# Seven products in place of eight in layer 0's channel MLP as well, with the order of its chunks changed

## The chip, the cores and the metric

The kernel runs on one core of a Trainium2 chip. Its engines work side by side, each through its own instructions in program order: TensorE (PE in the profile; its weight loads are PEld) multiplies, VectorE (DVE) and ScalarE (ACT) do the elementwise work, GpSimd (POOL) does nearly nothing here, and SyncE (SP) issues the DMAs. Operands lie in SBUF, matmul results in PSUM, everything large in DRAM. The metric is the device time of one execution in microseconds, shown as the median of three runs with the lowest and the highest.

## The reference, cut to what matters

Two layers; the first mixes with a spatial gating unit, the second with a pooling mixer. Both end in the same channel MLP, which is where the change lies.

```python
D_MODEL = 1024; SEQ = 1024; DEC_SEQ = 32; D_FF = 4 * D_MODEL
...
    for i in range(DEPTH):
        mod = jax.nn.silu(c) @ w_ada[i] + b_ada[i]
        sh1, sc1, gt1, sh2, sc2, gt2 = jnp.split(mod[:, None, :], N_MOD, axis=-1)
        h = rmsnorm(x, g_norm[i, 0]) * (1 + sc1) + sh1
...
        x = x + gt1 * rmsnorm(mix, g_norm[i, 1])
        h = rmsnorm(x, g_norm[i, 2]) * (1 + sc2) + sh2
        f = jnp.square(jax.nn.relu(h @ ffn_w_up[i])) @ ffn_w_down[i]
        x = x + gt2 * rmsnorm(f, g_norm[i, 3])
```

It runs for 1024 prompt frames and 32 sample frames that share the weights. All arrays are float32.

## The kernel before

**Tiles and splits.** Activations lie transposed, channels on the partitions, frames along the free axis, in three tiles: tiles 0 and 1 hold 384 prompt frames each, tile 2 the last 256 and the 32 sample frames, 288 columns. `acc[t]` holds a tile's residual stream. Every float32 operand is split in a high part (`wh`, `hh`, `fh`) and the remainder (`wl`, `hl`, `fl`), and each product is three matmuls: high by high, high by low, low by high (`products`, L923 to L925). ScalarE rounds the high part, VectorE subtracts for the low one. So a weight load of 128x1024 costs one activation (L419) and one VectorE subtraction, and each hidden block a relu, a square (ScalarE) and a split.

**The channel MLP** runs in chunks of 512 hidden features: `ffn_item` makes four up blocks `pf` (24 matmuls each) and leaves eight down blocks `pg` (12 each), which are issued after the next item's first up block (`pending`, `flush`). `accumulate` has VectorE add each `pg` to `acc`. After a tile's last chunk `Stat` sums squares for the next norm, and the caller's `after` starts a chain (`to_pool` after layer 0, `to_out` after layer 1).

**Seven products.** In layer 1 the last four chunks (`COMBINED = 4`) of tiles 0 and 1 are taken together by `combined_item`: a two-by-two scheme over even and odd blocks of channels and of hidden features, seven products of 12 matmuls (L1588) in place of eight, twice a chunk. It needs sums of the weights (`sh`, `sl`, made by `do_s`) and sums of the columns of the two tiles. The latter are made by `sums_of_columns` and `other_sums` out of the modulated activations that `mix_to_ffn` has stored in DRAM (`md`). They, and more hidden pieces, lie in the SBUF of tile 2's activations, in two of the sixteen weight slots (`W_SLOTS`, `w_cap`) and in borrowed buffers; `acc[2]` serves as scratch. When the last combined chunk's up products are issued, `late_modulation` loads tile 2 back from `md[2]` and remakes its `hh` and `hl`.

**The order of passes** (`passes`, L321 to L328). Layer 0: chunks 0 and 1 tile by tile, chunks 2 and 3 each over all three tiles with the weights loaded once, then chunks 4 to 7 of tile 0, of tile 1, of tile 2. Layer 1: chunks 0 to 3 of tile 0, of tile 1, the four combined ones, then all eight of tile 2.

**What else is woven in.** `fillers` is a queue of generators: the chains between the channel MLP and the next mixer (`ffn0_t`, `ffn1_t`, `out_t`) and the column sums. `weave`, called between blocks, pulls from the first two as long as a running estimate of VectorE's time (`time["dve"]`) is behind that of TensorE, and `finish` forces one to its end: `run_ffn` does so in front of a tile's first chunk. The modulation vectors come from `w_ada` by VectorE (`add_ada`, `add_wide`: scale and add into `aa`, transpose, reduce); these ada items stand in one stream with the weight loads, and `some_ada` says after which pass how many. The loop `for n, (l, c, tiles) in enumerate(passes)` puts twelve into each of layer 0's shared chunks and four into each of chunks 4 to 7 of tile 0. `stream_ready` holds a load back until there is a weight slot; from 24 loads in front of the first combined chunk (`wtight`) it counts `w_cap`, 14 slots, 16 after the last.

**The layers' border.** `to_pool(st)` appends `run`: the residual, scaling by `coef`, window sums, four groups of pooling matmuls `pp` (L2015) whose weights `wg` are loaded in front of each, and `mix_to_ffn`, whose `apply` makes eight scalings, `hh` and `hl`.

## Time and profile before

| | us |
|---|---|
| median of three runs | 2155.68 (2154.72 to 2156.45) |
| the profiled execution | 2157.29, its span 2155.4 |
| mean granted TensorE clock | 0.998 of full speed |

By stages, from the profile's windows (busy time in us):

| stage | from to | PE | DVE | ACT |
|---|---|---|---|---|
| norms and gating mixer | 0 to 577 | 571.86 | 392.65 | 224.31 |
| channel MLP of layer 0 | 577 to 1402 | 823.97 | 607.77 | 402.42 |
| layer 1, plain chunks of tiles 0 and 1 | 1402 to 1681.6 | 276.32 | 222.37 | 162.77 |
| its four combined chunks | 1681.63 to 1935.39 | 252.71 | 141.40 | 115.88 |
| tile 2 and the end | 1935.39 to 2155.4 | 210.02 | 144.33 | 111.20 |

A row of the windows gives start:end, length, the busy time of each engine with the number of instructions, the granted clock, the DMA share and GB/s. A row of the timeline gives start, duration, engine, line, operation, output and inputs, and in brackets the idle time before it and what ended it. Nearly every VectorE operation bears the line of one helper, L80, so it is told apart by its tiles. Matmuls are pipelined: a 384-column one lasts 0.33 us in the rows, and the next starts sooner. Line numbers are those of the kernel before.

### The profile page before, as it was taken

The numbers are of one execution on the slowest core, as the hardware profiler recorded it, in microseconds if no ns is written. First come the engines' busy times: TensorE is split into PE (matmuls) and PEld (weight loads), VectorE is DVE, ScalarE is ACT, GpSimd is POOL, SyncE is SP. The second block draws the span as 40 slices with busy tenths as digits, with TensorE's granted clock in tenths as the row PEclk, the third lists the DMA queues.
The fourth block names the chain that finished last, engine by engine and source line by source line (L and its number), as shares of the span: only waits on it lengthen the run. The fifth ranks groups of instructions, "written<-read, shape, count | busy, mean of one in ns | idle before, by whom it ended". The sixth has DMA issues, their size and how long they took to land.

```text
span 2155.4 us, 33342 instructions
## 1 busy us (share of the span) xinstructions
PE 2134.9 (99%) x13137; PEld 2060.1 (96%) x13137; DVE 1508.5 (70%) x2665; ACT 1016.6 (47%) x1738; POOL 15.3 (1%) x34
## 2 busy tenths in 40 slices
PE   9999999999999999999999999999999999999998
PEld 6778999999999999999999999999999999999998
DVE  6787748557778558486887868887858655479464
ACT  5534322234456552323345566666556443366454
POOL 0000000000000000000000000000000000001000
PEclk9999999999999999999999999999999999999999
DMA  8487524253447454243665546755556222158572
GB/s 307 147 266 214 164 86 127 86 161 107 135 120 225 126 151 147 87 138 115 198 187 152 163 143 210 221 171 177 156 172 188 79 69 69 40 164 228 146 204 79
DMA packets 393394, 330.02 MB, mean 153 GB/s; under 512 B 39986, under 2 KB 355930, under 8 KB 393236
## 3 DMA queue, kind: packets, MB, share of 16 engines
q1 hardware_dynamic: 392564, 326.99, 49.9%
q8 instruction: 103, 1.69, 0.3%
q0 software_dynamic: 640, 0.88, 0.1%
q14 instruction: 55, 0.45, 0.1%
q10 hardware_dynamic: 32, 0.01, 0.0%
HBM read 291.67 MB, written 36.17 MB: 152 GB/s over the span
## 4 chain that ended last, share of the span: by engine, by line
PE 87%; DVE 5%; DMA 4%; ACT 2%; issue 1%; SPq 0%; DVEq 0%; ACTq 0%
PE pg L923 10%; PE pg L925 10%; PE pg L924 10%; PE pf L923 8%; PE pf L924 8%; PE pf L925 8%; PE po L923 3%; PE po L925 3%; PE po L924 3%; PE pu L923 3%; PE pu L925 3%; PE pu L924 3%; PE pv L951 2%; PE pv L950 2%; PE pv L952 2%; PE pf_0a L1588 2%
## 5 line engine op out<-in xcount | busy, mean ns | idle before, releaser
L923 PE MATMUL pg<-fh,wh_dn 128*128 128x384 f32 (+1 forms) x1440 | 462.8, 322 | 0.2
L924 PE MATMUL pg<-fl,wh_dn 128*128 128x384 f32 (+1 forms) x1440 | 461.0, 320 | 1.7 <-DVE fl L80 1.5
L925 PE MATMUL pg<-fh,wl_dn 128*128 128x384 f32 (+1 forms) x1440 | 460.1, 320 | 0.0
L923 PE MATMUL pf<-hh,wh_up 128*128 128x384 f32 (+1 forms) x1280 | 409.2, 320 | 0.2 <-ACT r L1511 0.2
L924 PE MATMUL pf<-hl,wh_up 128*128 128x384 f32 (+1 forms) x1280 | 407.5, 319 | 0.8 <-DVE hl L80 0.8
L925 PE MATMUL pf<-hh,wl_up 128*128 128x384 f32 (+1 forms) x1280 | 407.3, 318 | 0.2 <-DVE wl_up L80 0.2
L924 PEld LDWEIGHTS pg<-fl,wh_dn 128*128 128x128 f32 x1440 | 270.3, 188 | 3.6 <-DVE fl L80 2.8
L923 PEld LDWEIGHTS pg<-fh,wh_dn 128*128 128x128 f32 x1440 | 270.2, 188 | 2.7 <-DVE acc L80 1.3
L925 PEld LDWEIGHTS pg<-fh,wl_dn 128*128 128x128 f32 x1440 | 270.2, 188 | 0.0
L80 DVE TENSOR_TENSOR wl_up<-raw,wh_up 128x1024 fp32r<-128x1024 f32 (+1 forms) x168 | 186.6, 1119 | 105.0 <-ACT wh_up L419 104.3
L80 DVE TENSOR_TENSOR acc<-acc,pg 128x384 f32<-128x384 f32 (+1 forms) x336 | 172.2, 517 | 111.6 <-PE pg L925 110.5
L419 ACT ACTIVATE wh_up<-raw 128x1024 fp32r<-128x1024 f32 x144 | 152.2, 1058 | 191.3 <-PE pf L924 118.7
L924 PEld LDWEIGHTS pf<-hl,wh_up 128*128 128x128 f32 x1280 | 240.2, 188 | 1.5 <-DVE hl L80 1.0
L925 PEld LDWEIGHTS pf<-hh,wl_up 128*128 128x128 f32 x1280 | 240.6, 188 | 0.6 <-DVE wl_up L80 0.6
L419 ACT ACTIVATE wh_dn<-raw 128x1024 fp32r<-128x1024 f32 x160 | 169.0, 1058 | 152.8 <-PE pg L924 101.9
L923 PEld LDWEIGHTS pf<-hh,wh_up 128*128 128x128 f32 x1280 | 240.0, 188 | 1.1 <-ACT r L1511 0.4
L80 DVE TENSOR_TENSOR wl_dn<-raw,wh_dn 128x1024 fp32r<-128x1024 f32 x160 | 195.4, 1222 | 58.2 <-ACT wh_dn L419 48.8
L80 DVE SCALAR_TENSOR_TENSOR aa<-raw,csil,aa 128x512 f32<-128x512 f32 (+1 forms) x364 | 203.2, 619 | 6.6 <-DMA raw<-in_w_ada_dram 6.5
L1511 ACT ACTIVATE r<-pf 128x384 f32<-128x384 f32 (+1 forms) x160 | 71.3, 446 | 176.6 <-PE pf L925 174.0
L923 PE MATMUL pu<-hh,wh_u 128*128 128x384 f32 (+1 forms) x384 | 125.8, 328 | 0.0
L923 PE MATMUL po<-ush,wh_o 128*128 128x384 f32 (+1 forms) x384 | 123.6, 322 | 0.0
L925 PE MATMUL pu<-hh,wl_u 128*128 128x384 f32 (+1 forms) x384 | 123.4, 321 | 0.0
(471 smaller groups left out, 3548.6 us busy)
## 6 DMA issues: line engine op xcount, KB each, us to landing
raw<-in_ffn_w_up_dram SPq DMA_DIRECT2D x160, 512.0 KB, 4.0
raw<-in_ffn_w_down_dram SPq DMA_DIRECT2D x160, 512.0 KB, 3.5
raw<-in_w_ada_dram SPq DMA_DIRECT2D x96, 512.0 KB, 4.5
raw<-in_sgu_w_in_dram SPq DMA_DIRECT2D x40, 512.0 KB, 4.2
xd<-acc SPq DMA_DIRECT2D x8, 1536.0 KB, 7.6
raw<-in_sgu_w_out_dram SPq DMA_DIRECT2D x24, 512.0 KB, 3.7
xo_r<-xd SPq DMA_DIRECT2D x32, 384.0 KB, 4.1
vd<-vt SPq DMA_DIRECT2D x32, 256.0 KB, 4.5
```

Source lines behind the costliest of these rows:

```text
L80: return op(out, *args, **kw)
L419: act(out=wh, in_=r, func=AF.Copy)
L923: mm(ps[:, :n], wh, rh, start=i == 0, stop=False)
L924: mm(ps[:, :n], wh, rl, start=False, stop=False)
L925: mm(ps[:, :n], wl, rh, start=False, stop=i == last)
L950: mm(ps[:m, :], a_h, wh[:, o : o + 512], start=k == 0, stop=False)
L951: mm(ps[:m, :], a_h, wl[:, o : o + 512], start=False, stop=False)
L952: mm(ps[:m, :], a_l, wh[:, o : o + 512], start=False, stop=k == KB - 1)
L1511: act(out=r[:, :n], in_=ps[:, :n], func=AF.Relu)
L1588: mm(ps[:, :n], u, v, start=first and k == 0 and x == 0, stop=k == 3 and x == 2, skip_group_check=True,)
```

## The change

Both layers now have a range of combined chunks, `COMBINED = [range(2, 6), range(4, 8)]`. In each layer tile 0 runs all its plain chunks, tile 1 those below the range, then come the combined ones, tile 1's chunks above the range, and tile 2's eight. In layer 0 that is tile 0: 0, 1, 6, 7; tile 1: 0, 1; both: 2 to 5; tile 1: 6, 7; tile 2: 0 to 7. In layer 1 the order is as it was. The twenty weight chunks of each layer stay twenty. `ends` says which pass is a tile's last, whatever its chunk number.

`mix_to_ffn` now stores the modulated activations in layer 0 too. `sums_of_columns` makes all four sums of columns, in the places where tile 0's `hh` and `hl` lay (the two tiles change roles in the products), once tile 0's plain chunks are issued (`plain`) and the chains of tiles 0 and 1 are done. Three weight slots are taken in place of two, and `aa` is no longer borrowed. A combined block waits for the second half of its weights only behind the first half of its first product. The remaining ada items move: two in each plain pass of tile 1 in layer 0, six in each combined chunk there, two in each of layer 1.

```diff
 W_SLOTS = 16
-COMBINED = 4
+COMBINED = [range(2, 6), range(4, 8)]
 RAW_SLOTS = 3
...
     every = list(range(NT))
-    passes = [(0, c, [t]) for t in every for c in (0, 1)]
-    passes += [(0, c, every) for c in range(2, 4)]
-    passes += [(0, c, [t]) for t in every for c in range(4, 8)]
     pair = every[:-1]
-    passes += [(1, c, [t]) for t in pair for c in range(8 - COMBINED)]
-    passes += [(1, c, pair) for c in range(8 - COMBINED, 8)]
-    combined = range(len(passes) - COMBINED, len(passes))
-    passes += [(1, c, [NT - 1]) for c in range(8)]
+    passes = []
+    runs = []
+    for l, cs in enumerate(COMBINED):
+        low, high = range(cs[0]), range(cs[-1] + 1, 8)
+        passes += [(l, c, [0]) for c in (*low, *high)] + [(l, c, [1]) for c in low]
+        runs.append(range(len(passes), len(passes) + len(cs)))
+        passes += [(l, c, pair) for c in cs]
+        passes += [(l, c, [1]) for c in high] + [(l, c, [NT - 1]) for c in range(8)]
+    ends = {(l, t): n for n, (l, _, tiles) in enumerate(passes) for t in tiles}
+    plain = set()
+    begun = set()
+    combined = [n for r in runs for n in r]
...
         w_chunk(n)
-        if l == 0:
-            some_ada(12 if len(tiles) > 1 else 4 if c >= 4 and tiles == every[:1] else 0)
+        if n in combined:
+            some_ada(2 if l else 6)
+        elif l == 0 and tiles == [1]:
+            some_ada(2)
     assert not rest
...
     wpos = {k: i for i, k in enumerate(worder)}
-    wtight = min(wpos[s[1]] for s in stream if s[0] == "s") - 24
+    wtight = [min(wpos[s[1]] for s in stream if s[0] == "s" and s[1][1] in r) - 24 for r in runs]
     wdone = set()
...
-    w_cap = [W_SLOTS - 2]
+    w_taken = [3, 3]
...
             i = wpos[stream[k][1]]
-            if i < wtight:
+            if stream[k][0] == "s" and passes[stream[k][1][1]][0] not in begun:
+                return False
+            if i < wtight[0]:
                 return i < W_SLOTS // 2 or worder[i - W_SLOTS // 2] in wdone
             used = sum(cost(key) for key in worder[:i] if key not in wdone)
-            return used + cost(worder[i]) <= w_cap[0]
+            return used + cost(worder[i]) <= W_SLOTS - max(
+                n for n, first in zip([0] + w_taken, [0] + wtight) if i >= first
+            )
         return True
...
                 flush()
-        if p + 1 == combined[0] and t == 1:
-            finish("ffn1_2")
-            fillers.append(("sums", other_sums()))
+        if t == 0 and passes[p + 1][2] != [0]:
+            plain.add(l)
         pending.append(down)
...
         def blocks(i):
-            w = [need_w(("up", p, i, q)) for q in range(2)]
-
-            def product(ps, first, a, b):
-                tick(12 * (0.004 + n / 2265.0))
-                for k in range(4):
+            w = [need_w(("up", p, i, 0))]
+
+            def product(ps, first, a, b, ks=range(4)):
+                tick(3 * len(ks) * (0.004 + n / 2265.0))
+                for k in ks:
                     q, m = divmod(k, 2)
...
             pa = ps_up(f"pf{p}_{i}a")
-            product(pa, True, 0, column(0, 0))
+            product(pa, True, 0, column(1, 0), range(2))
+            yield
+            w.append(need_w(("up", p, i, 1)))
+            product(pa, True, 0, column(1, 0), range(2, 4))
             u1 = copy(f"u1_{p}_{i}", pa)
...
             pb = ps_ms(f"pf{p}_{i}b")
-            product(pb, True, 1, column(0, 1))
+            product(pb, True, 1, column(1, 1))
             add(u1, pb)
-            finish_block(u1, None, 0, 2 * i)
+            finish_block(u1, None, 1, 2 * i)
             yield
...
             add(u4, pc)
-            finish_block(u4, None, 1, 2 * i + 1)
+            finish_block(u4, None, 0, 2 * i + 1)
             yield
-            product(pa, False, 6, column(1, 1))
-            finish_block(t_m(f"r_{p}_{i}"), pa, 1, 2 * i)
+            product(pa, False, 6, column(0, 1))
+            finish_block(t_m(f"r_{p}_{i}"), pa, 0, 2 * i)
             product(pc, False, 2, summed(3))
             add(u2, pc)
-            finish_block(u2, None, 0, 2 * i + 1)
+            finish_block(u2, None, 1, 2 * i + 1)
             for q in range(2):
...
                 accumulate(t, d, ps, False)
-                if d == 0 and after is not None:
+                if d == 0 and ends[l, t] == p:
                     st = Stat(t, f"rf{l}_{t}")
-                if after is not None:
+                if ends[l, t] == p:
                     st.square(d)
...
                 weave(d % 2)
-            if after is not None:
+            if ends[l, t] == p:
                 after(st)
...
         next(first)
-        finish("sums")
+        next(first)
         next(first)
...
         next(second)
+        next(second)
         weave()
         next(second)
-        if after is not None:
-            w_cap[0] = W_SLOTS
-            fillers.appendleft(("ffn1_2", late_modulation(NT - 1)))
+        done = p == runs[l][-1]
+        if done:
+            w_taken[l] = 0
+            fillers.appendleft((f"ffn{l}_2", late_modulation(l, NT - 1)))
         weave()
...
             down(t)
-            if after is not None:
-                finish("ffn1_2")
+            if done:
+                finish(f"ffn{l}_2")
...
         need_ada(l, 4)
-        if l == 0:
-            yield from modulate(out[0], l, 2, 3)
-            return
         got = []
...
         yield False
-        yield from sums_of_columns()
+        while l not in plain or any(f[0] in (f"ffn{l}_0", f"ffn{l}_1") for f in fillers):
+            yield 1.0
+        yield from sums_of_columns(l)
...
-    def sums_of_columns():
-        assert not any(f[0] in ("ffn1_0", "ffn1_1") for f in fillers)
+    def sums_of_columns(l):
+        begun.add(l)
         n = ncol[0]
...
             ("r", "rr", 2, [P, 384], 1),
-            ("a", "aa", 2, [P, 512], 1),
             ("w", "W", W_SLOTS, [P, 1024], 2),
         ):
-            for i in range(2 if tag == "W" else bufs):
+            for i in range(w_taken[l] if tag == "W" else bufs):
                 x = work.tile(shape, F32R, tag=tag, bufs=bufs, name=f"sums_{name}{i}")
...
         dsh = small.tile([P, 4], F32, tag="st", bufs=6, name="dshift")
-        sh = shift[:, 1, 1, :, 0].rearrange("p (k a) -> p k a", a=2)
+        sh = shift[:, l, 1, :, 0].rearrange("p (k a) -> p k a", a=2)
         tt(out=dsh, in0=sh[:, :, 1], in1=sh[:, :, 0], op=ALU.subtract)
         sums["dsh"] = dsh
-        for i in range(3):
-            yield from sum_columns(i, sums["spare"][2 * i : 2 * i + 2])
-
-    def other_sums():
-        homes = [(hh[1][:, 2 * i, :], hl[1][:, 2 * i, :]) for i in range(4)]
-        yield from sum_columns(3, homes[3])
-        for i in range(3):
-            for j, home in zip((0, 2), homes[i]):
-                hi, lo = sums["parts"][j, i]
-                act(out=home, in_=hi.bitcast(F32), func=AF.Copy)
-                sums["parts"][j, i] = home, lo
-            yield True
-        yield False
-
-    def sum_columns(i, homes):
+        for i in range(4):
+            yield from sum_columns(l, i, (hh[0][:, 2 * i, :], hl[0][:, 2 * i, :]))
+
+    def sum_columns(l, i, homes):
         n = ncol[0]
...
         t4 = t_m(f"sums_m{i}")
-        nc.sync.dma_start(t1, md[0][:, 2 * i, :])
+        nc.sync.dma_start(t1, md[1][:, 2 * i, :])
         nc.sync.dma_start(
-            scratch[:, 1408:2176].rearrange("p (a n) -> p a n", a=2), md[1][:, 2 * i : 2 * i + 2, :]
+            scratch[:, 1408:2176].rearrange("p (a n) -> p a n", a=2), md[0][:, 2 * i : 2 * i + 2, :]
         )
-        nc.sync.dma_start(t4, md[0][:, 2 * i + 1, :])
+        nc.sync.dma_start(t4, md[1][:, 2 * i + 1, :])
         yield 3.0
...
             (0, t1, None),
-            (1, t2, shift[:, 1, 1, 2 * i + 1, 0:1]),
+            (1, t2, shift[:, l, 1, 2 * i + 1, 0:1]),
             (3, t4, None),
...
-    def late_modulation(t):
+    def late_modulation(l, t):
         a = acc[t][:, :, HALO:]
         nc.sync.dma_start(a, md[t])
-        hh[t] = room("h", t, f"hh1_2_{t}", F32R)
-        hl[t] = room("l", t, f"hl1_2_{t}", F32R)
+        hh[t] = room("h", t, f"hh{l}_2_{t}", F32R)
+        hl[t] = room("l", t, f"hl{l}_2_{t}", F32R)
         yield 4.0
...
                 c = slice(c0, c0 + w)
-                b = shift[:, 1, 1, k, v : v + 1]
+                b = shift[:, l, 1, k, v : v + 1]
                 act(out=hh[t][:, k, c], in_=a[:, k, c], func=AF.Identity, bias=b, scale=1.0)
...
             if p in combined:
-                combined_item(p, after if c == 7 else None)
+                finish(f"ffn{l}_2")
+                combined_item(p, after)
                 continue
...
                     finish(f"ffn{l}_{t}")
-                ffn_item(p, t, after if c == 7 else None)
+                ffn_item(p, t, after if ends[l, t] == p else None)
```

## The prediction

> **What bounds the kernel now.** I read the page's busy times first, then the chain of work that ended last, then the span by windows.
>
> ```profile
> span 2155.4 us, 33342 instructions
> PE 2134.9 (99%) x13137; PEld 2060.1 (96%) x13137; DVE 1508.5 (70%) x2665; ACT 1016.6 (47%) x1738; POOL 15.3 (1%) x34
> PE 87%; DVE 5%; DMA 4%; ACT 2%; issue 1%; SPq 0%; DVEq 0%; ACTq 0%
> ```
>
> TensorE is busy in 99% of the span and carries 87% of the chain; VectorE has 30% of the span free and ScalarE 53%. So time falls only where matmuls go or where one of TensorE's rare waits goes, and it rises where something makes TensorE wait. The next rows (start:end, length, then busy time of PE, PEld, DVE, ACT, POOL, the granted clock, the DMA share, GB/s) are the stages on which everything below rests.
>
> ```profile
> core 0: us, PE busy (x) PEld busy (x) DVE busy (x) ACT busy (x) POOL busy (x), PEclk, DMA share, GB/s
> 670.36:703.64 33.28, 33.28 (x193) 33.28 (x193) 28.12 (x50) 18.03 (x29) 0.00 (x0) 1.00 0.73 224
> 821.36:913.75 92.39, 92.39 (x587) 92.11 (x585) 64.04 (x103) 25.60 (x44) 0.00 (x0) 1.00 0.38 114
> ...
> 1040.00:1075.00 35.00, 34.16 (x203) 33.42 (x202) 30.47 (x46) 13.87 (x20) 0.00 (x0) 1.00 0.64 193
> 1681.63:1744.72 63.09, 63.05 (x361) 62.43 (x361) 34.34 (x63) 25.47 (x46) 0.00 (x0) 1.00 0.22 67
> 1744.72:1807.81 63.09, 63.04 (x361) 62.42 (x361) 34.30 (x63) 25.47 (x46) 0.00 (x0) 1.00 0.22 67
> ...
> 1870.89:1935.39 64.50, 63.60 (x364) 62.73 (x364) 38.42 (x60) 39.46 (x76) 0.00 (x0) 1.00 0.44 133
> 1372.00:1402.00 30.00, 30.00 (x199) 30.00 (x199) 19.12 (x30) 17.79 (x30) 0.00 (x0) 1.00 0.58 179
> 1651.00:1681.60 30.60, 29.79 (x170) 29.15 (x169) 29.41 (x57) 18.90 (x36) 0.00 (x0) 1.00 0.53 162
> 1935.39:1955.00 19.61, 17.30 (x126) 16.73 (x126) 19.61 (x40) 10.91 (x20) 0.00 (x0) 1.00 0.69 193
> ```
>
> The first is one plain chunk of a 384-column tile: 4 x 24 up matmuls and 8 x 12 down matmuls, 192 in 33.28 us, 173.3 ns each, no wait. The second is layer 0's chunk 2 over all three tiles with its twelve modulation (ada) items: VectorE works 64.04 of 92.39 us and TensorE does not wait. The two rows at 1681 and 1744 are the seven-product chunks that layer 1 has already. The last rows are layer 1's start (no wait), the stage in front of its first combined chunk (0.81 us idle), its last combined chunk (1.41 us longer than the others) and the stage behind it (2.31 us idle).
>
> **Part 1, seven products in place of eight.** A plain chunk of tiles 0 and 1 has 2 x 96 = 192 up matmuls. A combined one has 2 blocks x 7 products x 12 = 168. Four chunks lose 96 matmuls, and the built order of the two programs agrees: 96 matmuls of 128x384 fewer, none of 288 columns. 96 x 173.3 ns = **-16.64 us**. A combined chunk has 168 + 192 = 360 matmuls, 62.39 us at that pitch, and took 63.09, so it pays 0.70 us of its own: **+2.8 us** for four. The fourth of layer 1 paid 1.41 more. Its end reloads the third tile from DRAM and makes sixteen extra ScalarE activations there (ACT 39.46 against 25.47 us); the new layer 0 has the same reload at the same place, yet in the built order the hidden pieces that TensorE waits for stand ahead of those activations: +0.7, half of 0 to 1.4.
>
> **Part 2, modulation items.** Forty of them moved: six in each combined chunk of layer 0, two in each of tile 1's four plain chunks there, two in each combined chunk of layer 1. What one costs VectorE follows from the two shared chunks, 24 items in 821 to 1007 us (count, busy time, mean ns):
>
> ```profile
> L80 DVE SCALAR_TENSOR_TENSOR aa<-raw,csil,aa 128x512 f32<-128x512 f32 x86 | 59.3, 748 | 0.4 <-DMA raw<-in_w_ada_dram 0.4
> L546 DVE STREAM_TRANSPOSE raw<-aa 128x512 f32<-128x512 f32 x12 | 7.8, 689 | 0.0
> L549 DVE TENSOR_REDUCE sums<-raw 128x32 f32<-128x1024 f32 x6 | 7.3, 1212 | 0.0
> L80 DVE TENSOR_SCALAR aa<-raw,csil 128x512 f32<-128x512 f32 x14 | 6.4, 474 | 0.7 <-DMA raw<-in_w_ada_dram 0.7
> ```
>
> (59.3 + 7.8 + 7.3 + 6.4) / 24 = 3.37 us. A combined chunk of layer 0 then has 34.34 + 6 x 3.37 = 54.6 us of VectorE work in 63.09, 86%. The row at 1040 is the nearest in share, 30.47 of 35.00 (87%), with 0.84 us idle; the row at 821, 69%, has none. Bounds for four chunks: 0 and 4 x 0.84 x 63 / 35 = 6.0. I take **+1.0**, nearer to nothing, because the adds that free a PSUM bank have some 1.7 us in hand in the built order. The items that caused the 0.84 us at 1040 are gone from there: -0.8 (-1.3 to 0). Layer 1's combined chunks rise to 34.34 + 6.7 = 41 of 63 us and lose one more of the sixteen weight slots: +0.5 (0 to 3).
>
> **Part 3, sums and the way into layer 0's combined chunks.** The column sums are now made twice, during tile 1's plain chunks ahead of them: 16 more loads on SP's queue, ScalarE and VectorE work under matmuls. Layer 1's entry has 0.81 us idle with VectorE at 29.41 of 30.60. Bounds 0 and 1.4; I take +0.5, as two chunks of 33.28 us lie over the work. If that cover were gone, the whole last set of sums would stand bare, like the wait priced next.
>
> **Part 4, the start of layer 1.** This is the new wait. Before, the built order had tile 0's pooling matmuls in front of the last four chunks of layer 0, and its modulation was long done when layer 1 began (row at 1372: no idle). Now tiles 0 and 1 end layer 0 two chunks apart, their chains share VectorE's spare time in tile 2's eight short chunks, tile 0's pooling matmuls stand among the chunks 5 and 6, and its last stretch falls behind tile 2's last down product (call its end T0): on VectorE an add, three adds of squares and three weight remainders (queued there for the next chunk), the scaled sum, two steps of the inverse root, then eight scalings and eight low halves `hl`; the first 48 matmuls of layer 1 wait for these one by one. Start-to-start times come from VectorE's timeline:
>
> ```profile
> 1934.90 0.61 DVE L80 SCALAR_TENSOR_TENSOR acc<-acc,coef,r_rf 128x384 f32<-128x384 f32 x1
> 1935.43 0.55 DVE L80 TENSOR_TENSOR sq_rf<-sq_rf 128x384 f32<-128x384 f32 x1
> 1935.90 4.55 DVE L80 SCALAR_TENSOR_TENSOR hl<-acc,shift,hh 128x256 fp32r<-128x256 f32 x16
> 1940.37 0.55 DVE L80 TENSOR_TENSOR acc<-acc,pg 128x384 f32<-128x384 f32 x1
> 1940.84 1.22 DVE L80 TENSOR_TENSOR wl_dn<-raw,wh_dn 128x1024 fp32r<-128x1024 f32 x1
> 1942.04 1.22 DVE L80 TENSOR_TENSOR wl_up<-raw,wh_up 128x1024 fp32r<-128x1024 f32 x1
> 1943.19 0.55 DVE L80 TENSOR_TENSOR sq_rf<-sq_rf 128x384 f32<-128x384 f32 x1
> ...
> 1944.54 0.62 DVE L80 SCALAR_TENSOR_TENSOR sm_rf<-sq_rf,eps,sc_rf 128x384 fp32r<-128x384 f32 x1
> 1945.07 1.22 DVE L80 TENSOR_TENSOR wl_up<-raw,wh_up 128x1024 fp32r<-128x1024 f32 x1
> ```
>
> Scaling 0.53 us, add 0.47, remainder 1.20 and 1.15, scaled sum 0.53. An operation on 288 columns lasts 0.45 to 0.46:
>
> ```profile
> L80 DVE TENSOR_TENSOR acc<-acc,pg 128x288 f32<-128x288 f32 x112 | 49.8, 450 | 29.4 <-PE pg L925 29.1
> L80 DVE TENSOR_TENSOR sq_rf<-sq_rf 128x288 f32<-128x288 f32 x12 | 5.5, 456 | 3.0 <-ACT sq_rf L771 2.6
> ```
>
> less the same 0.08 of overlap, 0.38. Sum: 4 x 0.38 + 3 x 1.15 + 0.45 = 5.4 to the scaled sum, 1.0 for the root, 16 x 0.53 = 8.5: the last `hl` at T0 + 14.9. Eight matmuls follow (1.4): T0 + 16.3. Without waits the four small matmuls and the 48 would end at T0 + 8.9. So **+7.5 us**. Lower bound 5, if the remainders were queued earlier and VectorE met T0 with nothing else to do (three remainders of 1.15 less, some of it already hidden); upper bound 11, when T0 finds VectorE some 2 us behind and the clock falls (third rival). Nothing hides it: every engine is waiting on VectorE here, and TensorE runs in program order.
>
> [...]
>
> **Part 5, what stays.** Weight loads are the same twenty chunks a layer; the way out of layer 1's combined chunks keeps its order; the pooling matmuls come at other moments:
>
> ```profile
> 1563.99 3.83 PE L2015 MATMUL pp<-acc,wg 128*128 128x288 f32 x8 [1.95 <-DMA wg<-in_pool_w_grp_dram]
> ```
>
> and, by windows,
>
> ```profile
> 1564.00:1566.00 2.00, 2.00 (x5) 1.52 (x6) 0.00 (x0) 0.00 (x0) 0.00 (x0) 0.59 0.91 284
> ...
> 1550.00:1585.00 35.00, 33.00 (x166) 29.96 (x165) 17.88 (x38) 19.95 (x38) 0.00 (x0) 0.95 0.47 139
> ```
>
> Their weights are loaded right in front of them, and one of the three tiles waited 1.95 us. That may go or come again: 0, bounds -3.5 and +3.5.
>
> **The sum:** -16.6 + 2.8 + 0.7 + 1.0 - 0.8 + 0.5 + 0.5 + 7.5 = -4.4 us. The profiled execution took 2157.3 us, span 2155.4 and 1.9 around it; 2152.9 is left. Its own time stood 1.6 above the median of the three runs, 2155.68, so against the median **2151.3, called 2151**. This kernel's measurement tells apart some 0.2%, 4.3 us, so the forecast lies just at that line.
>
> **Rivals.**
>
> *The waits turn out small* (22%). For it: layer 1 shows entry, chunks and exit with 0.8, 0.7 and 2.3 us only. Against: the built order puts the remainders in front. With the lower bound 5 at layer 1's start and nothing for parts 2, 3 and the fourth chunk: -16.6 + 2.8 + 5 - 0.8 = -9.6, 2146.
>
> *VectorE decides in layer 0's combined chunks* (20%, the slower side). VectorE works in order; a bank of PSUM is freed by its add, and up to four ada operations of 0.75 us can stand in front of that add. Five such adds a chunk, each late by 0.75 us, make 3.7 us a chunk, 15 for four, in place of my 1.0: 2165; with three adds late, 2159. It decides from about 2.5 us a chunk on. For it: 86% busy with no stretch off. Against: the row at 821, where ada items run as densely (12 in 92 us) beside 64.04 us of work.
>
> *The clock falls at the start of layer 1* (10%). After the wait of 1.95 us above, the granted clock was 0.59 in the next two microseconds; over the 35 us around it the mean is 0.95, so 0.05 x 35 = 1.75 us went. The wait at layer 1 leaves TensorE bare for some 5 us. The same 1.75 us there, part of it under VectorE's pace, and some 2 us of lateness of VectorE at T0 with it: 2154. [...]
>
> *The change does not do what it says* (3%): the built order counts the 96 matmuls away, so only a measurement near 2155.7 with the same matmul count would say so.
>
> **How the numbers follow.** The forecast itself has 45%: its own range is 2146 to 2156, 28 of it below 2151.4 (faster by over 0.2%; the terms of parts 2 and 3 are all taken above their lower bound, nothing) and 17 within. Faster: 28 + 22 = 50%. Same: 17 + 8 of the clock's 10 + 3 = 28%. Slower: 20 + the other 2 = 22%. The range reaches from the full saving with no new wait in the chunks and the pool wait gone (2146 - 3.5, and part of the start's bound, 2141) to the middle of the slower rival, 2162.
>
> **What would show it.** Right: 96 matmuls fewer; four stretches in layer 0 of 63 to 64 us with VectorE near 55; one gap of 6 to 9 us in front of layer 1's first up matmuls, ended by `hl` of VectorE; no idle where 1040 to 1075 lay. Wrong: combined chunks of 65 us or more in layer 0, waits for `acc` or `wl` inside them, a start of layer 1 without the gap, or a new wait in front of the first combined chunk above 1.4 us.

## The result, and the profile after

The changed kernel takes 2164.68 us, median of six runs (2163.81 to 2165.08), against 2156.06 (2154.72 to 2159.64) of the kernel before beside it: ratio 1.0036, 95% interval 1.0024 to 1.0049, so 8.6 us slower. Forecast was 2151. (The table of stages ahead of the prediction lets layer 0's channel MLP begin at 577 us; its first up matmul stands at 619 in both kernels. No number below depends on it.)

The page of the changed kernel, its span, its busy times and the summary of its chain:

```profile
span 2163.3 us, 33333 instructions
PE 2128.3 (98%) x13041; PEld 2046.8 (95%) x13041; DVE 1569.6 (73%) x2818; ACT 1041.6 (48%) x1804; POOL 15.3 (1%) x34
PE 82%; DMA 6%; DVE 6%; ACT 4%; issue 1%; SPq 0%; DVEq 0%; ACTq 0%
```

The matmuls went as forecast: 13041 in place of 13137, 96 fewer. VectorE got 61 us of work more, and what left the chain at TensorE (87% before, 82% now) came back at DMA, VectorE and ScalarE. Windows of the changed kernel show where: the four combined chunks of layer 0, the start of layer 1, two of the combined chunks of layer 1.

```profile
833.71:898.29 64.58, 64.11 (x369) 62.46 (x369) 50.99 (x92) 26.12 (x46) 0.00 (x0) 1.00 0.37 116
898.29:962.25 63.96, 63.35 (x362) 62.42 (x361) 52.15 (x89) 26.05 (x46) 0.00 (x0) 1.00 0.35 107
962.25:1027.03 64.78, 63.93 (x370) 62.48 (x369) 52.23 (x96) 26.29 (x46) 0.00 (x0) 1.00 0.39 120
1027.03:1091.10 64.07, 63.63 (x369) 62.49 (x369) 50.14 (x81) 33.90 (x66) 0.00 (x0) 1.00 0.51 158
...
1360.00:1400.00 40.00, 33.12 (x201) 31.27 (x200) 34.45 (x55) 22.85 (x41) 0.00 (x0) 0.91 0.53 166
1380.00:1382.00 2.00, 0.62 (x2) 0.34 (x2) 2.00 (x4) 0.23 (x1) 0.00 (x0) 0.84 0.86 247
1382.00:1384.00 2.00, 0.26 (x1) 0.00 (x0) 1.93 (x5) 1.07 (x3) 0.00 (x0) 0.50 0.83 216
...
1386.00:1388.00 2.00, 2.00 (x8) 2.00 (x8) 2.00 (x5) 1.49 (x3) 0.00 (x0) 0.50 0.07 21
1388.00:1390.00 2.00, 2.00 (x13) 2.00 (x13) 2.00 (x5) 0.50 (x2) 0.00 (x0) 0.96 0.00 0
...
1746.81:1810.55 63.74, 63.16 (x361) 62.42 (x361) 41.71 (x75) 25.56 (x46) 0.00 (x0) 1.00 0.28 84
1810.55:1874.79 64.24, 63.14 (x362) 62.43 (x362) 39.13 (x72) 24.99 (x46) 0.00 (x0) 1.00 0.26 82
```

A combined chunk has 360 matmuls and 62.39 us at the pitch, the time from one matmul's start to the next where nothing waits. Layer 0's four took 257.39 us, 7.8 above it (0.5 of that are thirty small matmuls among them); layer 1's two here 1.35 and 1.85 above it, where those before paid 0.70. In front of layer 1's first matmuls TensorE is idle for 6.9 of 40 us, and it then runs at a granted clock of 0.50 until 1388. What TensorE waited for between 833 and 1945 us, by the view of waits (total, times, longest):

```profile
PE pg L934 <- ACT sums_l L1347: 5.8, 8, 1.3
PE pn_rf L827 <- ACT sc_rf L812: 3.4, 1, 3.4
PE pg L934 <- ACT fh L1347: 2.5, 1, 2.5
```

To add this up I take, for every matmul, the time to the next one's start less the pitch (173.3 ns for 384 columns, 131.8 for 288; the pooling's matmuls, 322 ns for 384 columns, and the other forms, 227 ns for 512 columns and 112 for 128, follow one another at paces of their own in both traces and count by these), and sum it by stage. The sums depend on that choice by some tenths of a microsecond. Halved clocks are in it. "Tail" is all that stands behind layer 1's combined chunks. The last column is what the prediction's terms come to.

| stage | before | after | more | forecast |
|---|---|---|---|---|
| up to 690 us | 18.95 | 19.29 | +0.3 | 0 |
| 690 us to layer 0's combined chunks | 0.30 | 0.52 | +0.2 | +0.5 |
| those chunks (before: the shared ones) | 2.76 | 7.27 | +4.5 | +3.7 |
| their exit, to 1300 us | 2.13 | 2.97 | +0.8 | 0 |
| start of layer 1, 1300 to 1405 us | 0.39 | 12.03 | +11.6 | +7.5 |
| layer 1's plain chunks with the pooling | 8.14 | 5.54 | -2.6 | 0 |
| the last 40 us before its combined chunks | 1.37 | 4.41 | +3.0 | 0 |
| its combined chunks | 3.85 | 7.26 | +3.4 | +0.5 |
| tail | 6.14 | 9.25 | +3.1 | 0 |
| sum | 44.0 | 68.5 | +24.5 | +12.2 |

24.5 less 16.64 is 7.9, the difference of the spans (2163.3 and 2155.4).

**The start of layer 1** went through the chain that was forecast. First three rows of TensorE's timeline, then VectorE's, both of the changed kernel; the last down product ends at 1376.1 (T0):

```profile
1379.87 0.40 PE L827 MATMUL pn_rf<-sc_rf,ones 128*128 128x288 f32 x1 [3.42 <-ACT sc_rf L812]
1381.65 0.61 PE L827 MATMUL pn_rf<-sm_rf,ones 128*128 128x288 f32 x1 [1.38 <-DVE sm_rf L80]
1384.01 1.01 PE L934 MATMUL pf<-hh,wh_up 128*128 128x384 f32 x2 [1.75 <-ACT hh L907]
```

```profile
1377.30 1.23 DVE L80 TENSOR_TENSOR wl_dn<-raw,wh_dn 128x1024 fp32r<-128x1024 f32 x1
...
1378.80 2.36 DVE L80 TENSOR_TENSOR wl_dn<-raw,wh_dn 128x1024 fp32r<-128x1024 f32 x2
1381.07 0.52 DVE L80 SCALAR_TENSOR_TENSOR sm_rf<-sq_rf,eps,sc_rf 128x288 fp32r<-128x288 f32 x1
...
1382.69 1.68 DVE L80 SCALAR_TENSOR_TENSOR acc<-acc,coef,r_r_0x 128x384 f32<-128x384 f32 x3
...
1390.34 1.15 DVE L80 SCALAR_TENSOR_TENSOR hl<-acc,shift,hh 128x384 fp32r<-128x384 f32 x2 [0.16 <-ACT hh L907]
```

Three weight remainders, the scaled sum, the root, sixteen operations of 0.53 us: the last `hl` ends at 1391.5, T0 + 15.4, where T0 + 14.9 was forecast. The gap comes in three pieces, and what ends the last is `hh` of ScalarE, not `hl`. The remaining difference is the clock: TensorE was nearly idle from 1376.5 to 1384.0 (7.5 us above the pitch) and then ran its next matmuls at half clock until 1388.2 (2.2 us more).

**Inside the combined chunks** the waits stand at the turn to the down products. VectorE, then ScalarE, then TensorE of the changed kernel:

```profile
1050.58 2.73 DVE L80 SCALAR_TENSOR_TENSOR aa<-raw,csil,aa 128x512 f32<-128x512 f32 x4
1053.23 1.22 DVE L80 TENSOR_TENSOR wl_dn<-raw,wh_dn 128x1024 fp32r<-128x1024 f32 x1
1054.36 0.54 DVE L80 TENSOR_TENSOR acc<-acc,pf_1c 128x384 f32<-128x384 f32 x1
```

```profile
1054.94 0.53 ACT L1582 ACTIVATE acc<-acc 128x384 f32<-128x384 f32 x1 [2.15 <-DVE acc L80]
...
1056.05 0.53 ACT L1347 ACTIVATE sums_l<-acc 128x384 fp32r<-128x384 f32 x1
```

```profile
1058.12 0.44 PE L934 MATMUL pg<-sums_l,wh_dn 128*128 128x384 f32 x1 [0.44 <-ACT sums_l L1347]
```

Four modulation operations and a remainder stand ahead of the add that completes the block; ScalarE waits 2.15 us for that add and has the next block's hidden pieces queued behind it; TensorE waits for those pieces. The wait for the modulation item passes through two engines before TensorE shows it, and there it bears ScalarE's name.

### The profile page after: what moved, and what is told of

The parts are those of the page before. It is cut to its first block, busy times and chain, and to the rows that moved or that the text cites. A ratio compares the mean times of both kernels' runs of the same rounds, so it can differ in the third digit from the quotient of the medians.

```text
span 2163.3 us, 33333 instructions
## 1 busy us (share of the span) xinstructions
PE 2128.3 (98%) x13041; PEld 2046.8 (95%) x13041; DVE 1569.6 (73%) x2818; ACT 1041.6 (48%) x1804; POOL 15.3 (1%) x34
## 4 chain that ended last, share of the span: by engine, by line
PE 82%; DMA 6%; DVE 6%; ACT 4%; issue 1%; SPq 0%; DVEq 0%; ACTq 0%
PE pg L934 10%; PE pg L935 10%; PE pg L936 10%; PE pf L934 6%; PE pf L935 6%; PE pf L936 6%; DMA raw<-in_w_ada_dram 3%; PE po L934 3%; PE po L936 3%; PE po L935 3%; PE pf_0a L1598 3%; PE pu L934 3%; PE pu L936 3%; PE pu L935 3%; PE pv L961 2%; PE pv L962 2%
## 5 line engine op out<-in xcount | busy, mean ns | idle before, releaser
L934 PE MATMUL pg<-fh,wh_dn 128*128 128x384 f32 (+1 forms) x1344 | 432.2, 322 | 2.6 <-ACT fh L1347 2.5
L935 PE MATMUL pg<-fl,wh_dn 128*128 128x384 f32 (+1 forms) x1344 | 430.3, 320 | 0.1
L936 PE MATMUL pg<-fh,wl_dn 128*128 128x384 f32 (+1 forms) x1344 | 429.6, 320 | 0.1
L934 PE MATMUL pf<-hh,wh_up 128*128 128x384 f32 (+1 forms) x1024 | 324.4, 318 | 4.3 <-ACT r L1522 2.5
L936 PE MATMUL pf<-hh,wl_up 128*128 128x384 f32 (+1 forms) x1024 | 322.9, 316 | 1.5 <-DVE wl_up L80 1.3
L935 PE MATMUL pf<-hl,wh_up 128*128 128x384 f32 (+1 forms) x1024 | 323.1, 316 | 0.1
L80 DVE SCALAR_TENSOR_TENSOR aa<-raw,csil,aa 128x512 f32<-128x512 f32 (+1 forms) x364 | 205.8, 621 | 14.9 <-DMA raw<-in_w_ada_dram 14.9
L934 PEld LDWEIGHTS pf<-hh,wh_up 128*128 128x128 f32 x1024 | 192.7, 188 | 6.0 <-ACT r L1522 3.0
L936 PEld LDWEIGHTS pf<-hh,wl_up 128*128 128x128 f32 x1024 | 193.3, 189 | 2.4 <-DVE wl_up L80 2.4
L935 PEld LDWEIGHTS pf<-hl,wh_up 128*128 128x128 f32 x1024 | 192.9, 188 | 1.3 <-DVE hl L80 0.9
L935 PE MATMUL pu<-hl,wh_u 128*128 128x384 f32 (+1 forms) x384 | 123.6, 322 | 0.0
```

The lines of the kernel that those rows point to most:

```text
L80: return op(out, *args, **kw)
L934: mm(ps[:, :n], wh, rh, start=i == 0, stop=False)
L935: mm(ps[:, :n], wh, rl, start=False, stop=False)
L936: mm(ps[:, :n], wl, rh, start=False, stop=i == last)
```

## The experiments

Each kernel is the changed one with the edit shown, timed against runs of the kernel before on the same chip.

**1. Tile 0's chain forced to its end one chunk earlier.** This takes away the late stretch in front of layer 1 and leaves the rest.

```diff
+                if l == 0 and t == NT - 1 and c == 7:
+                    finish("ffn1_0")
                 ffn_item(p, t, after if ends[l, t] == p else None)
```

> The changed kernel with tile 0's chain to layer 1 forced to its end in front of tile 2's last chunk of layer 0. Theory A (the wait at layer 1's start is the serial tail of this chain and the halved clock behind it): the 10.5 us there fall below 2, up to 2 come back inside tile 2's last chunk, 2156 us (2153 to 2159). Rival C (VectorE has too much to do in that stage, so the wait only moves): 2162 to 2165, with waits of 6 us or more in tile 2's last chunk or behind it.

2158.53 us (2155.76 to 2160.95), ratio 1.0006 (0.9997 to 1.0016). The same window as above:

```profile
1360.00:1400.00 40.00, 38.55 (x255) 38.32 (x254) 36.19 (x50) 26.60 (x42) 0.00 (x0) 1.00 0.76 227
```

The granted clock is back at 1.00, and the 12.0 us that the stage from 1300 to 1405 stood above the pitch are 5.2; what is left lies in tile 2's last chunk, in waits for a ScalarE piece (1.4 us) and a bank-freeing add (1.1). 6.2 us of the 8.6 are gone with the one edit, within the expected range, although more stayed in the stage than the 4 us expected at most. Layer 0's combined chunks keep 7.1, layer 1's 7.6.

**2 and 3. No modulation items in any combined chunk**, alone and with edit 1; the items go to the plain chunks of layer 0.

```diff
-        if n in combined:
-            some_ada(2 if l else 6)
-        elif l == 0 and tiles == [1]:
-            some_ada(2)
+        if l == 0 and n not in combined:
+            some_ada(1 if tiles == [NT - 1] else 4)
```

> The changed kernel with no ada item in any combined chunk: the same 40 items stand four in each plain chunk of tiles 0 and 1 of layer 0 and one in each of tile 2's eight. Theory A (ada operations stand ahead of VectorE's bank-freeing adds, ScalarE waits for these in order, the last hidden pieces come late): layer 0's four combined chunks fall from 257.4 us to 252.5, layer 1's four by 3 us, the plain chunks lose 0 to 2, so 2157 us (2155 to 2160). Rival B (the pieces are late because the two tiles changed roles and the weights come by halves, whatever ada does): the chunks keep 64 us and more, 2163 to 2165.

> Both edits together. Theory A: the two gains add, 2148 us (2145 to 2152), faster than the kernel before. Rivals B and C: 2155 or more.

2212.28 us (2209.01 to 2214.1), ratio 1.025 (1.0235 to 1.0265), and 2203.9, ratio 1.0218 (1.0202 to 1.0234): both forecasts missed by over 50 us. The third combined chunk of layer 0 and the wait in front of the first one, run 2:

```profile
999.99:1062.72 62.73, 62.73 (x361) 62.44 (x361) 34.49 (x64) 25.12 (x46) 0.00 (x0) 1.00 0.22 68
```

```profile
PE pf_0a L1596 <- ACT wh_up L466: 19.9, 1, 19.9
```

Without the items the chunk costs 0.34 us above the pitch, no more: the seven products with their exchanged roles and the split wait for the weights are innocent. But with four items in each of tile 1's plain chunks the column sums end late, and the first combined chunk waits for its weights, whose splitting stands behind the sums on ScalarE. That is the bare last set of sums which the prediction named as the price of a lost cover, and it is 20 us. It is not the whole loss: from 690 us to that chunk run 2 stands 34 us above the pitch, these 20 among them (0.5 in the changed kernel), and layer 1's plain chunks more than 20 (5.5); the other waits were not followed.

**4. The changed order with eight products in layer 0.** Chunks 2 to 5 run as pairs of tiles that share their weights; no sums, no seven products in layer 0; items as in the changed kernel.

```diff
-    combined = [n for r in runs for n in r]
+    combined = list(runs[1])
...
-        if n in combined:
+        if len(tiles) > 1:
             some_ada(2 if l else 6)
...
-    w_taken = [3, 3]
+    w_taken = [0, 3]
...
         need_ada(l, 4)
+        if l == 0:
+            yield from modulate(out[0], l, 2, 3)
+            return
```

> The changed order with eight products in layer 0: chunks 2 to 5 of tiles 0 and 1 share their weights but run as plain chunks, six ada items each, and no column sums are made in layer 0. Theory A: 96 matmuls come back (+16.6), and the overhead of 7.8 us in the four combined chunks, their entry and exit (2 us) goes; the start of layer 1 keeps its 10 us: 2171 us (2168 to 2174). Rival D (the seven products gain nothing in layer 0 as built, all of the loss is theirs): 2163 to 2166.

2158.55 us (2156.81 to 2161.48), ratio 1.0005 (0.9996 to 1.0015), 6.1 faster than with seven products, where 6 slower was expected. The four chunks that run as pairs, in one window:

```profile
833.70:1091.10 257.40, 257.40 (x1504) 256.55 (x1503) 165.54 (x254) 85.35 (x139) 0.00 (x0) 1.00 0.37 111
```

No idle, with the same 24 items as the changed kernel has there. Against this run the changed kernel stands 22.9 us higher above the pitch: 6.6 in layer 0's chunks, 10.2 at the start of layer 1, 4.1 in front of its combined chunks, 2.1 in its plain ones, 0.8 on both sides of layer 0's chunks, and 0.8 less elsewhere. That is the price of the seven products of layer 0, for 16.64 us of matmuls. It also shows what they don't cause: layer 1's combined chunks (7.4 here) and the tail (10.3) lose as much without them.

**5. Edit 1, and layer 1's eight items moved ahead**, two into each of tile 1's plain chunks of layer 1.

```diff
-            some_ada(2 if l else 6)
-        elif l == 0 and tiles == [1]:
+            some_ada(0 if l else 6)
+        elif tiles == [1]:
             some_ada(2)
```

> Run e2 (tile 0's chain ahead of tile 2's last chunk) with the eight ada items of layer 1's combined chunks moved into tile 1's four plain chunks there, two each; layer 0 keeps its six a chunk. Theory A (ada operations ahead of the freeing adds make the last hidden pieces late): layer 1's four combined chunks lose 3 us of their 7 us of overhead, layer 0's stay at 64 us each; 2155.5 us (2153 to 2158) against e2's 2158.5. Rival B (role change and half weights): layer 1's chunks stay at 64 us, 2158 or more.

2164.85 us (2163.54 to 2165.91), ratio 1.0029 (1.0018 to 1.0041). Layer 1's second chunk, and the wait in front of its first:

```profile
1750.41:1813.13 62.72, 62.72 (x361) 62.46 (x361) 34.47 (x64) 25.11 (x46) 0.00 (x0) 1.00 0.22 68
```

```profile
PE pf_0a L1598 <- ACT wh_up L468: 12.8, 1, 12.8
```

The chunk is clean (0.33 above the pitch), so the items are what layer 1's chunks pay for; and again the entry takes it over, as in runs 2 and 3: the first chunk, behind its late start, pays some 5 us.

**6 and 7. VectorE relieved by GpSimd.** Run 6 gives GpSimd the window additions of the pooling, run 7 (with edit 1) the differences of the column sums as well.

```diff
                         lo += step
-                        tt(
+                        nc.gpsimd.tensor_tensor(
```

> The changed kernel with the window sums of the pooling (ten additions a tile) on GpSimd, nothing moved in the program. Theory A (VectorE has no time left between 1190 and 1330 us, so tile 0's chain ends behind tile 2's last product): VectorE is rid of 10 us a tile, the wait at layer 1's start falls from 10.5 us to below 6 and the entry of layer 1's combined chunks from 4.4 to below 3; 2158 us (2155 to 2162). Rival E (the chain's own length decides, and GpSimd takes longer for each addition): 2164 or more.

> Run e2 with the window sums and the four differences of each set of column sums on GpSimd. Theory A: VectorE's load falls by 30 us for the windows and 18 for the sums, the waits of e2 in tile 2's last chunk (3.2), at the entries (0.8 and 2.4) fall by half or more: 2153 us (2150 to 2157), faster than the kernel before by 0.1%. Rival E (longer chains, or GpSimd slows VectorE): 2158 or more.

2184.27 us, ratio 1.0118 (1.0103 to 1.0133), and 2202.55, ratio 1.0205 (1.019 to 1.0221). Groups of run 6 between 1090 and 1700 us, then the same two groups of VectorE in the changed kernel:

```profile
L80 DVE TENSOR_TENSOR wl_dn<-raw,wh_dn 128x1024 fp32r<-128x1024 f32 x72 | 91.3, 1271 | 28.0 <-ACT wh_dn L426 22.4 <-PE pg L935 4.2 <-PE pf L935 1.0
...
L1966 POOL TENSOR_TENSOR win1p<-acc 128x798 f32<-128x798 f32 x4 | 8.3, 2064 | 74.7 <-ACT r L1524 72.2 <-DVE acc L80 2.4
```

```profile
L80 DVE TENSOR_TENSOR wl_dn<-raw,wh_dn 128x1024 fp32r<-128x1024 f32 x75 | 91.5, 1223 | 24.1 <-ACT wh_dn L426 23.8
...
L80 DVE TENSOR_TENSOR win1p<-acc 128x798 f32<-128x798 f32 x4 | 3.9, 982 | 0.0
```

The addition of 0.98 us takes 2.06 on GpSimd, and VectorE's own remainders go from 1.223 to 1.271 us on the mean. The mean hides what happens: of run 6's 141 remainders there (`wl_dn` and `wl_up`, 91.3 and 87.7 us) the thirteen that run beside a GpSimd addition take 1.76 us on the mean, all others 1.22. The chains that wait for the windows get longer (VectorE waits 3.3 us for `win1p` there), and the relief is more than lost.

**8 and 9. Layer 1's items still earlier** (four behind chunk 1 of tile 0, four behind chunk 0 of tile 1, with edit 1), and in run 9 tile 0's chain forced before chunk 6.

```diff
-            some_ada(2 if l else 6)
+            some_ada(0 if l else 6)
+        elif (l, c, tiles) in ((1, 1, [0]), (1, 0, [1])):
+            some_ada(4)
```

> Run e2 with layer 1's eight last ada items earlier in the stream than in e5: four behind chunk 1 of tile 0 and four behind chunk 0 of tile 1 in layer 1, none in or right ahead of its combined chunks. Theory A, now with the stream's order in it (an ada item hurts where it stands ahead of work that TensorE needs next: ahead of a freeing add in a combined chunk, or ahead of the weights of the first combined chunk): layer 1's four combined chunks have 0.4 us of overhead each as in e5, the entry stays below 3 us, 2154 us (2151 to 2157). If ada items cost wherever they stand: 2158 or more.

> Run e8 with tile 0's chain forced to its end one chunk earlier, in front of tile 2's chunk 6. Theory A: the 3.2 us that e2 still lost in tile 2's last chunk go, up to 3 come in chunk 6, as the four pooling products are then issued together: equal to e8 within 2 us. Rival C (VectorE's backlog only moves): 3 us slower than e8 or more.

2185.61 us, ratio 1.0126 (1.0113 to 1.014), and 2192.92, ratio 1.0162 (1.0148 to 1.0176). In both the first combined chunk of layer 1 waits 27.8 us for its weights, where an entry below 3 us was expected; the second and the third are clean (0.4 us each). Layer 1's plain chunks have no room for eight items in any place tried while the same stretch must make the column sums.

**10 to 12. Is it the items' work that holds the chunks?** Run 10 leaves three of four scale-and-add operations of each such item out; runs 11 (alone) and 12 (with edit 1) leave out all VectorE operations of these items that read a load, and keep the loads. Parts of the modulation vectors are not computed in these three.

```diff
+                if state["next"] in short and c + v > 0 and (q > 0 or c > 0):
+                    time["dve"] += 0.16 + w / 840.0
+                    continue
...
+                if skip:
+                    time["dve"] += 0.16 + w / 840.0
+                    continue
```

> The changed kernel, but every modulation item in a combined chunk of either layer runs one of its four scale-and-add operations (two for the first item of a set) and leaves the rest out, so part of the modulation vectors of layers 0 and 1 is not computed; loads, waits for them, transposes, reductions and matmuls stay, and the order of the rest nearly so. 92 operations of 0.75 us, 69 us of VectorE, fall away out of the eight combined chunks. Theory (the items' own VectorE time in front of the bank-freeing adds makes the pieces late): layer 0's four combined chunks fall from 257.4 us to about 252 (excess over the matmul pitch from 7.8 to 2 or 3), layer 1's from 7.1 to 3 or 4 above the pitch, the start of layer 1 keeps its 9 to 11 us since no item lies near it; in all 2155, ratio to before 0.9995. Rival A (waiting for the items' loads, not their work, holds VectorE; or the exchanged roles of the tiles and the split wait for the weights cost it): the chunks stay within 2 us of what they were, 2163 to 2165. Rival B (VectorE's load in the combined chunks also sets the start of layer 1): that wait shrinks by 4 us or more, 2150.

> The changed kernel, but no modulation item in a combined chunk of either layer runs any VectorE operation that reads its load: the scale-and-add operations, transposes and reductions are left out, zeros stand in for the sums, so part of the modulation vectors is not computed. The items' loads keep their places on SP's queue and the planned order stays nearly the same. So VectorE has neither their work nor a wait for their loads there. Theory (VectorE runs in order, and an item's operation that stands ahead of a hidden piece's add holds it back whether by its work or by the wait for its load; in the last pair of runs the shortened items waited 15.3 us for loads in layer 0's combined chunks): the waits at the turn to the down products go, layer 0's four chunks fall to 2 to 3 us above the matmul pitch in all (7.3 in the changed kernel), layer 1's to 2 to 3 (7.7); layer 1's start keeps its 10; in all 2155. Rival (the loads themselves, on SP's queue and in the three raw slots, make weights late, or the combined chunks cost this by their roles and slots): the chunks stay within 2 us of what they were, 2162 or more.

> The same part left out, in the kernel with tile 0's chain forced to its end in front of tile 2's last chunk of layer 0 (2158.5 alone). Theory: the two costs stand at separate places and add up, 2150, ratio 0.997. Rival (VectorE's or ScalarE's lateness moves on to the next place, as in every version so far that freed one): the chunks are clean but new waits of 4 us or more stand at layer 1's entry, start or end, 2155 or more.

Run 10: 2167.38 us, ratio 1.0044 (1.003 to 1.0058), not better than the changed kernel although VectorE has 55 us less to do (1514.9 against 1569.6). Layer 0's four chunks stand 11.5 us above the pitch. Its waits of VectorE in layer 0's chunks, then those of the changed kernel:

```profile
DVE aa L80 <- DMA raw<-in_w_ada_dram: 15.3, 12, 3.5
```

```profile
DVE aa L80 <- DMA raw<-in_w_ada_dram: 6.2, 6, 1.6
```

And two rows of run 10, of VectorE and of TensorE behind it:

```profile
1060.00 0.75 DVE L80 SCALAR_TENSOR_TENSOR aa<-raw,csil,aa 128x512 f32<-128x512 f32 x1 [1.34 <-DMA raw<-in_w_ada_dram]
1060.67 0.55 DVE L80 TENSOR_TENSOR sums_c<-r,sums_l 128x384 fp32r<-128x384 f32 x1
```

```profile
1061.28 0.69 PE L941 MATMUL pg<-sums_c,wh_dn 128*128 128x384 f32 x1 [1.22 <-DVE sums_c L80]
```

VectorE, done earlier, waits at the same place for the item's load, with the hidden piece `sums_c` behind it, and TensorE waits for the piece. My theory (that the work alone holds the chunks) falls. Rival A, the wait for the load, has the direction, but layer 0's chunks lost 4.2 us more instead of staying within 2. The same edit with edit 1 besides was run too: 2159.62 us (2158.47 to 2163.54), ratio 1.0017 (1.0008 to 1.0026), where 2150 was expected and edit 1 alone took 2158.53; layer 0's chunks stand at 10.0 us there. Run 11: 2157.83 us (2153.34 to 2162.04), ratio 1.0002 (0.9993 to 1.0011). VectorE and TensorE there:

```profile
871.84 0.43 DVE L80 TENSOR_TENSOR acc<-raw 128x256 f32<-128x256 f32 x1 [6.42 <-DMA raw<-in_ffn_w_up_dram]
872.19 0.55 DVE L80 TENSOR_TENSOR acc<-acc,pf_1c 128x384 f32<-128x384 f32 x1
```

```profile
873.92 0.69 PE L949 MATMUL pg<-fh,wh_dn 128*128 128x384 f32 x1 [3.07 <-DVE acc L80]
```

With no item left to wait for, VectorE waits 6.42 us for the next load in the stream, the weights whose sum it makes, and again an add that frees a bank is behind it; layer 0's chunks stand at 20.4 us, worse than with the items, where 2 to 3 was expected. So the loads alone are enough to make the chunks late, which was the rival. The items' loads hold up the queue: SyncE waits 46.9 us in this stretch for them to land before it can issue the next (7.6 in the changed kernel). The planned order slid here, so that the pooling of tile 0 came early (at 1275 us, 1298 in the changed kernel) and the start of layer 1 has no wait; that, and not the reason expected, is why the time is near that of before. The rows are of an execution of 2162.04 us. Run 12, 2159.27 us (ratio 1.0008, 1.0 to 1.0017), has 14.6 us in these chunks. These runs leave one reading, which no single run isolates: what decides is where the operations that read a load stand in VectorE's order, and when the load lands. The weights and the items come through three buffers, in one order; a load is issued when a buffer comes free, and in layer 0's combined chunks of the changed kernel it lands 3.2 to 6.0 us later, 3.8 in the median. In the changed kernel itself both parts stand ahead of the adds, the 2.73 us of item work shown above and a wait for the load (6.2 us in all of layer 0's chunks). A fourth buffer was not tried.

**13 and 14. The items in layer 0 alone.** Run 13 is run 4 (eight products) with eight items in each pair chunk of layer 0 and none in layer 1's combined chunks; run 14 the same placement with seven products and edit 1.

```diff
-            some_ada(2 if l else 6)
+            some_ada(0 if l else 8)
```

> The run with eight products in layer 0 again (its chunks 2 to 5 of tiles 0 and 1 as pairs that share weights), with eight modulation items in each pair chunk of layer 0 and none in layer 1's combined chunks. Those chunks stood 7.4 us above the matmul pitch there, layer 0's pair chunks 0.7 us with VectorE at 165.5 of 257.4 us. Theory (the items alone hold layer 1's chunks, and layer 0's pairs have room for eight more, 27 us): layer 1's chunks fall to 2 to 3.5 us above the pitch, layer 0's pairs rise by less than 1.5, 2154 to 2155, 0.1% below before. Rival (what is freed there comes back elsewhere, as in each version so far): 2157 to 2159.

> Seven products in both layers, tile 0's chain forced to its end in front of tile 2's last chunk of layer 0 (2158.5 with six and two items), and now eight modulation items in each combined chunk of layer 0 and none in layer 1's. Theory (items cost by their place: 7.1 us above the pitch in layer 0's four chunks for 24 items, of which some 1.5 are the chunks' own, so 0.23 us an item; 7.6 in layer 1's for 8 items, of which 2.7 are its own as the last run showed, 0.6 an item): 4 to 5 us gained in layer 1, 2 lost in layer 0, 2156, ratio 0.9995. If so the seven products of layer 0 still cost 4 us against the same placement with eight products (2152). Rival (VectorE has no room for two more items a chunk: 34.3 + 8 x 3.4 = 61.3 of 63 us): layer 0's chunks lose 8 us or more, 2162 or above.

Run 13: 2151.95 us (2150.33 to 2153.71), ratio 0.9975 (0.9964 to 0.9985) against 2156.6 of before beside it: faster than both kernels. Layer 0's pairs and layer 1's first combined chunk:

```profile
833.70:1091.10 257.40, 257.40 (x1510) 256.26 (x1509) 188.68 (x293) 85.15 (x137) 0.00 (x0) 1.00 0.43 127
1676.81:1739.57 62.76, 62.76 (x362) 62.46 (x362) 34.51 (x64) 25.12 (x46) 0.00 (x0) 1.00 0.23 68
```

Layer 1's chunks are clean (1.7 us for four) and the pairs of layer 0 hold 32 items at no cost, VectorE at 188.68 of 257.40 us (73%). Run 14: 2181.03 us, ratio 1.0111 (1.0094 to 1.0128), 29 us worse for the same placement, and slower than the 2156 expected by 25. Its combined chunks don't lose more (6.6 us), against the rival's wording, but the lateness comes out behind them: 12.4 us up to 1300, 10.9 at the start of layer 1, 18.3 in layer 1's plain chunks, with 8.9 at one norm's sum. VectorE is busy for 226.80 of the 257.40 us there, 88%. So the likely reading is that VectorE's backlog in layer 0 decides whether its seven products pay; no placement of the items tried lets them pay.

## Why the prediction was wrong

**Right:** the 96 matmuls; that the start of layer 1 is the largest new wait, with its chain and its end (T0 + 15.4 for T0 + 14.9); that on VectorE the next operation starts before the one ahead has ended (0.53 us from start to start where one lasts 0.61, in the three scalings at 1382.69); the way in (+0.2 for +0.5); and, by luck, the sum over layer 0's stage, +4.5 for +3.7, which came from two errors: the chunks stood 7.3 above the pitch where 4.5 was forecast, and what the shared chunks of before gave back was 2.8 and not 0.8.

The forecast of -4.4 us became +7.9, a miss of 12.3: 4.1 of it at the start of layer 1, 2.9 in layer 1's combined chunks, 3.0 at their entry and 3.1 in the tail; the rest, with the pooling's waits in it, sums to -0.8.

**The start of layer 1, mis-sized** (part 4: 7.5, bounds 5 to 11; measured +11.6 from 1300 us on, +10.4 from 1360 on). The chain was half a microsecond longer than forecast. The halved clock, which I had left to a rival with 10%, cost 2.2 us by itself and belonged in the forecast, since the row at 1564 had already shown a fall, to 0.59, behind a wait of 1.95 us, and this wait was known to be longer: its first gap is 3.42 us. A wait of 2.53 us, below, is followed by a fall too. The last 1.2 us lie in tile 2's chunks before 1360.

**Layer 1's combined chunks, the wrong step** (part 2: +0.5; measured +3.4, run 5 and run 13 show it gone with the items). I priced an item by the share of VectorE that is busy, 41 of 63 us, and found it harmless. An item costs by its place: operations that wait for a load or work on it, ahead of one add. With two items a chunk and VectorE busy for 65% of it, layer 1's chunks above pay 1.0 and 1.5 us more than the 0.33 of run 5; with six items at 80%, layer 0's pay some 1.5. The share alone doesn't decide: run 13's pairs of eight products, at 73% and with eight items each, stand 0.9 us above the pitch in all. The rival "VectorE decides in layer 0's combined chunks" had this place right (items ahead of the bank-freeing adds), but priced it too high, at 15 us for four chunks or some 9 with three adds late, where some 6 came; it did not say that layer 1 pays as well, nor that waits take the place of the work when the work goes.

**Part 5, set to nothing, the wrong step:** the entry of layer 1's combined chunks, +3.0, and its mechanism is the same on ScalarE. Rows of the changed kernel, the last two of them windows:

```profile
1662.69 0.94 ACT L468 ACTIVATE wh_up<-raw 128x512 fp32r<-128x512 f32 x2 [0.61 <-DMA raw<-in_ffn_w_up_dram]
1664.47 0.42 ACT L468 ACTIVATE wh_up<-raw 128x256 fp32r<-128x256 f32 x1 [0.84 <-DMA raw<-in_ffn_w_up_dram]
1664.79 0.47 ACT L1522 ACTIVATE r<-pf 128x384 f32<-128x384 f32 x1
```

```profile
1667.23 0.45 PE L934 MATMUL pg<-fh,wh_dn 128*128 128x384 f32 x1 [2.53 <-ACT fh L1347]
```

```profile
1668.00:1670.00 2.00, 2.00 (x9) 2.00 (x8) 2.00 (x6) 0.80 (x3) 0.00 (x0) 0.52 0.70 220
1670.00:1672.00 2.00, 2.00 (x9) 2.00 (x8) 2.00 (x5) 1.07 (x2) 0.00 (x0) 0.63 0.06 20
```

ScalarE waits for two loads with the relu of a finished block behind them, and TensorE waits 2.53 us for that block. Behind the wait the granted clock falls again, to 0.52 and 0.63 in the next two windows. That takes 0.48 and 0.37 of 2 us each, 1.7 us of the entry's 4.4. The wait is absent in run 4 (0.3), whose items stand in the same places, so the seven products of layer 0 bring it about, hundreds of microseconds behind their own chunks; the path between was not followed. With seven products it is absent as well where TensorE has lost more time before it: the entry stands at 0.1 to 0.3 in runs 2, 3, 6, 7 and 14. The tail's +3.1 was set to nothing too; run 4 has it without layer 0's seven products (10.3), run 5 and run 13 without items in layer 1's combined chunks (8.7 and 8.6). Its longest new wait has the same form, rows of ScalarE and TensorE of the changed kernel:

```profile
2108.00 1.06 ACT L426 ACTIVATE wh_up<-raw 128x1024 fp32r<-128x1024 f32 x1 [1.69 <-DMA raw<-in_ffn_w_up_dram]
```

```profile
2109.41 0.40 PE L934 MATMUL pf<-hh,wh_up 128*128 128x288 f32 x1 [2.16 <-ACT r L1522]
```

The relu `r` stands behind the split that waits for its load, and TensorE waits for the relu; in the tail of before such a wait lasted 0.2 us. Why the load comes late there, and the rest of the +3.1, stays open. The pooling's waits took -2.6 back, within the bounds given.

The common fault: the terms were priced each in its own stage, against VectorE's mean share there. Runs 4 and 14 show that the seven products of layer 0 cost time in stages behind it: 29 us lie between runs 14 and 13, seven and eight products with one placement of the items (run 14 has edit 1 besides). The likely carrier is the 61 us added to VectorE; the path was not followed from stage to stage.

## What to carry to other kernels

Work that reads a load, put into the queue of an engine that also frees the banks, cost here by what was queued behind it and by when the load landed, not by the engine's busy share: look for the add or the relu behind it, before the share. A saving on the busiest engine that is paid with work on the second one has to be priced over the whole stretch until the second has caught up; there try the cheaper placement without the saving first, which here gave 0.25% while the saving itself lost 0.4%.

## What the runs showed of the hardware

That 55 us of VectorE's work could go and nothing be gained (run 10) had not been expected: VectorE waited 6.42 us for the load at the head of its queue (run 11) with an add behind it whose product was done at 865.3, 6.5 us before the load came; ScalarE waited 0.61 and 0.84 us for loads (the changed kernel, rows at 1662.69 and 1664.47) with the relu of a block behind them that was done at 1661.9. The granted clock fell to 0.84 and 0.50 in the windows after an idle stretch of 3.42 us and was full again at 1388.2, 4.2 us after matmuls resumed; a wait of 2.53 us at 1664.7 was followed by a fall as well, to 0.52 and 0.63; the 2.16 us wait in the tail was not (1.00 from 2109 to 2113 us). With the window additions on GpSimd, VectorE's own remainders took 4% longer on the mean, and those beside an addition 44% longer (1.76 us for 1.22).
